# Constant products on TensorE before the first tile of x, the identity on SP's queue, and the norm's scale ahead of the weighted product at the end of a hybrid decoder layer

## The chip, the cores and the metric

The kernel runs on one core of one Trainium2 chip. The metric is the device time of one execution in microseconds. Before the change it is 662.05 us, the median of 3 runs (661.96 to 663.56).

A core has five engines that each work through their own list of instructions in order: TensorE (PE; its weight loads are shown as PEld), VectorE (DVE), ScalarE (ACT), GpSimd (POOL) and SyncE (SP), which here only issues DMAs. They wait for one another by semaphores.

## The reference

The layer has 512 rows of 1024 values in float32. What matters here is its first and last step:

```python
h = rms_norm(x, pre_mix_norm[l])
proj = jnp.einsum('bsd,dc->bsc', h, w_in[l])
...                       # MoBA attention and gated DeltaNet, output projection
x = x + rms_norm(mix, post_mix_norm[l])
h = rms_norm(x, pre_mlp_norm[l])
m = jnp.einsum('bsf,fd->bsd', jnp.square(jax.nn.relu(jnp.einsum('bsd,df->bsf', h, w_up[l]))), w_down[l])
x = x + rms_norm(m, post_mlp_norm[l])
```

with `rms_norm(x, w) = x * rsqrt(mean(x*x) + EPS) * w`. In the DeltaNet part, `exp(A_log)` enters the decay `g`.

## The kernel before

Every float32 factor of a large product is split into a high part (`hi`, a cast by ACT to a format that TensorE reads at one pass) and a low part (`lo`, the difference, by DVE or POOL); a product is then three matmuls, `hi*hi`, `hi*lo`, `lo*hi` (`mm3`).

**The start** (`pre_norm`). x comes in four tiles of 128 rows, 512 KB each (`take(0)` to `take(3)`, tensor `xx`). SP issues, in this order: x tile 0, the norm's weights (`pre_mix`, one row), x tile 1, two blocks of `w_in`, x tile 2, two more blocks of `w_in` (into `nb`), x tile 3, and then small constants, among them `alg` (`a_log`, line 312). The identity matrix that the transposes need is loaded by POOL (line 201). At most eight DMAs of SP are under way: each waits for the one eight before it.

TensorE first spreads the row of weights over 128 partitions, by a product with a row of ones (two matmuls into `ps_a`, the buffers `nb`). For each tile of x, ACT squares and sums the rows (line 214), POOL makes the root (`rstd_of`, lines 168 and 172), DVE scales by root and weights (line 220, `xs`), TensorE transposes eight 128x128 blocks (line 81, `ps_g`), ACT casts the high part out of PSUM (line 110, `hT_h`) and DVE subtracts to give the low part (line 111, `hT_l`), for two halves of the columns each. The scaling of tiles 0 and 1 stands ahead of the low parts of both in DVE's order. `ps_g` has three buffers, so the second half of tile 1 needs the first half of tile 0 to be done.

The projections (`projections`) begin with 48 matmuls for the first 256 rows: 24 for each of two output blocks. The weights for the second output block (`first_w[2]`, `first_w[3]`) are split after tile 2 and tile 3 of x have been squared: ACT's cast, and DVE's or POOL's subtraction (line 135). After that tiles 2 and 3 of x are transposed.

The order on TensorE is written out by `Weave`, which runs the stages as generators, counts up an estimated time `now` with every matmul, and starts a stage when its due time is reached (`START`, `WAIT`). In the first stage the order of ACT, DVE and POOL is held to the program's (`in_order`); between those, and later, a scheduler that simulates the engines places the other instructions. One of these is the exponential `ea<-alg` on ACT (line 466), which belongs to the DeltaNet's scalars and whose result is used later.

**The end.** The last product, of the MLP, is accumulated in PSUM. For each 128 rows `t` and half `b` of the columns, `half(b, t)` sums the squares on ACT (line 1308) and multiplies by the norm's weights `nb3` on DVE (line 1310 or 1312, result `Y(t, b)`). `normed_y(t)` adds the two sums (DVE, line 1316) and makes the root on POOL (lines 168, 172). `finish(t)` calls it if it has not been called, multiplies by the root, adds the residual (DVE, line 1326, twice) and issues the DMA of the output. Here the order of all engines is the program's (`ordered`). For the last two tiles computed (t = 0 and 1) the code is

```python
        half(1, j)
        finish(j)
```

so the order on DVE is: weighted product, sum, and the two final operations.

Of the kernel before, what the change touches and what calls it, by code (L numbers as in the profile page):

```python
# [20 lines left out]

RANK = {'chunks': 5, 'inverse': 3, 'scan': 3, 'scores': 4, 'values': 2, 'finish_o': 1, 'take': 4}
LEAD = {'chunks': 0, 'inverse': 100, 'scan': 100, 'scores': 0, 'values': 100, 'finish_o': 0, 'take': 0, 'take_a': 0}
START = (5.5, 9.0, 17, 16, 30, 10.5)
ORDER = "q0 k0 x0 k1 q1 q2 k2 k3 z0 q3 y0 x1 v0 w0 v1 y1 w1 v2 x2 v3 x3 y2 w2 y3 z1 w3 z2 z3"


class Weave:
# [10 lines left out]
    def spawn(self, rank, stream, lead=0):  # L39
        self.live.append([rank, self.now, stream, lead])  # L40
        self.live.sort(key=lambda s: s[0])

    def mark(self, name, wait=0.0):
        self.marks[name] = self.now + wait
# [22 lines left out]
def layer(ctx, tc, nc, x, w_in, w_ab, w_out, w_up, w_down, conv_w, a_log, dt_bias, gdn_norm_w, rel_bias,  # L67
# [8 lines left out]
    def mm(o, l, r, **kw):  # L76
        nc.tensor.matmul(o, l, r, **kw)  # L77
        weave.now += math.prod(r.shape[1:]) * (1 if r.dtype == FR else 4) / 2400

    def transpose(o, i, k=128):  # L80
        nc.tensor.transpose(o, i, ident[:k, :k])  # L81
        weave.now += k * 4 / 2400
# [18 lines left out]
    def big(name, shape=(128, 4, 512), dt=FT):  # L101
        return apool.tile(list(shape), dt, name=name, tag="big", bufs=14)
# [6 lines left out]
    def split(hi, lo, src):  # L109
        nc.scalar.copy(hi, src)  # L110
        tt(lo, src, f32(hi), op=OP.subtract)  # L111
# [20 lines left out]
    def ended(w, sub=None):  # L132
        hi, lo, raw, v = w
        nc.scalar.copy(hi, raw)  # L134
        (sub or tt)(lo, raw, f32(hi), op=OP.subtract)  # L135
        return v(hi), v(lo)
# [10 lines left out]
    ident = const.tile([128, 128], FT, name="ident")  # L147
# [7 lines left out]
    def bank(tag="g", shape=(128, 512)):  # L155
        return psum.tile(list(shape), FT, name="ps_" + tag, tag=tag, bufs={"mm": 2, "g": 3, "a": 3}[tag])
# [10 lines left out]
    def rstd_of(r, ss, n):  # L167
        nc.gpsimd.tensor_scalar(r, ss, 1.0 / n, EPS, op0=OP.mult, op1=OP.add)  # L168
        m = mhalf[:, :math.prod(r.shape[1:])]
        if len(r.shape) == 3:  # L170
            m = m.rearrange("p (a b) -> p a b", a=r.shape[1])
        nc.gpsimd.tensor_tensor(r, r, m, op=OP.pow)
        return r
# [3 lines left out]
    def bias_in():  # L177
        he = at.tile([128, 1280], FT, name="L")
        hot, es = he[:33, :640], he[:8, 640:]
        nc.sync.dma_start(hot, c_hot)  # L180
        rb = at.tile([33, 8], FT, name="rb", bufs=1)
        nc.vector.memset(rb, -1e30)
        nc.sync.dma_start(rb[:32], rel_bias)
        return hot, es, rb


    def pre_norm(ahead):
        one = tmp("one")[:1, :128]
        nc.vector.memset(one, 1.0)
        in_order.enter_context(tc.manual_schedule(engines={mybir.EngineType.Activation, mybir.EngineType.DVE, mybir.EngineType.Pool}))  # L190
        xx = [big("xx", (128, 2, 1024)) for _ in range(2)]
        nrow = nb0[:1]
        sqs = big("xs0", (128, 2, 1024))
        nb = [bank("a") for _ in range(2)]

        def take(t):
            nc.sync.dma_start(xx[t // 2][:, t % 2], x[128 * t:128 * t + 128, :])

        take(0)
        nc.sync.dma_start(nrow[:, :1024], pre_mix[None, :])  # L200
        nc.gpsimd.dma_start(ident, c_ident)
        take(1)
        ahead()
        take(2)
        ahead()
        take(3)
        rel.extend(bias_in())
        for b in range(2):
            mm(nb[b], one, nrow[:, 512 * b:512 * b + 512], start=True, stop=True)
        mark("x")  # L210

        def sumsq_x(t):
            ss = const.tile([128, 1], FT, name=f"ss{t}")
            act(sqs[:, t % 2], xx[t // 2][:, t % 2], AF.Square, accum_out=ss)
            return rstd_of(ss, ss, 1024)

        def scaled(t, r):
            for b in range(2):
                bs = slice(512 * b, 512 * b + 512)
                stt(sqs[:, t % 2, bs], xx[t // 2][:, t % 2, bs], r, nb[b], op0=OP.mult, op1=OP.mult)  # L220

        r = [sumsq_x(t) for t in range(2)]
        ahead()
        for t in range(2):
            scaled(t, r[t])
        for t in range(4):
            yield max(0, START[t] - weave.now)
            for b in range(2):
                tp = bank("g")
                for j in range(4):  # L230
                    transpose(tp[:, 128 * j:128 * j + 128], sqs[:, t % 2, 512 * b + 128 * j:512 * b + 128 * j + 128])
                v = tp.rearrange("p (a b) -> p a b", a=4)
                split(hT_h[b][:, :, 128 * t:128 * t + 128], hT_l[b][:, :, 128 * t:128 * t + 128], v)
            mark(f"h{t}", WAIT["h"])
            if t == 1:
                r = sumsq_x(2)
                first_w[2] = ended(first_w[2])
                scaled(2, r)
                r = sumsq_x(3)
                first_w[3] = ended(first_w[3], nc.gpsimd.tensor_tensor)  # L240
                scaled(3, r)
# [7 lines left out]
    def projections(items):  # L249
# [13 lines left out]
        for t in (0, 2):  # L263
# [5 lines left out]
            for i, ps in enumerate(first):  # L269
# [3 lines left out]
                if t:  # L273
                    spawn(RANK["take"], items[i][1](ps), LEAD["take"])
                yield 0
        W = [third, load(5)]
        for n in range(4, 2 * len(items)):
# [8 lines left out]
            for j in range(4):  # L286
                k = 4 * (n % 2) + j
                mm3(ps, hi[:, j], lo[:, j], kof(hT_h, k), kof(hT_l, k), k == 0, k == 7)
                if k == 7:
                    spawn(RANK["take"], ev(ps), LEAD["take_a" if col < 1536 else "take"])  # L290
                yield 0
# [6 lines left out]
    def tmp(name, dt=FT):  # L298
        return gpool.tile([128, 512], dt, name=name, tag="tmp", bufs=4)
# [9 lines left out]
    def constants_in():  # L309
        nc.sync.dma_start(cw, conv_w)  # L310
        nc.sync.dma_start(dtb, dt_bias.partition_broadcast(128))
        nc.sync.dma_start(alg, a_log.partition_broadcast(128))
        yield START[5]
        nc.vector.tensor_scalar(cw, cw, 0.5, None, op0=OP.mult)
# [271 lines left out]
    def bias():  # L586
        hot, es, rb = rel
        yield max(0, START[4] - weave.now)
        for a, b in ((0, 512), (512, 640)):
# [145 lines left out]
    def scan():  # L735
# [65 lines left out]
        for t in range(4):  # L801
# [38 lines left out]
            yield WAIT["state"]  # L840
            spawn(RANK["finish_o"], finish_o(t, o), LEAD["finish_o"])
        mark("scan")
# [4 lines left out]
    def finish_o(t, o):  # L847
        sq = tmp2("osq")
        act(sq, o, AF.Square)
        ss = sc.tile([128, 8], FT, name="oss")  # L850
        e8 = lambda a: a.rearrange("p (h e) -> p h e", h=8)
        nc.vector.tensor_reduce(ss, e8(sq), axis=mybir.AxisListType.X, op=OP.add)
        nc.gpsimd.tensor_tensor(ss, ss, rq2[:, t], op=OP.mult)
        r = rstd_of(ss, ss, 64)
        nc.gpsimd.tensor_tensor(r, r, rq8[:, t], op=OP.mult)
        tt(e8(o), e8(o), r[:, :, None].to_broadcast([128, 8, 64]), op=OP.mult)
        yield WAIT["o_in"]
        for p in range(4):
            yield f"z{p}"
        tp = bank(shape=(128, 4, 128))  # L860
        for p in range(4):
            transpose(tp[:, p], o[:, 128 * p:128 * p + 128])
        ts = slice(128 * t, 128 * t + 128)
        m = tmp2("om").rearrange("p (a b) -> p a b", a=4)
        stt(m, tp, nw, zss[0][:, :, ts], op0=OP.mult, op1=OP.mult)
        split(mx_h[1][:, :, ts], mx_l[1][:, :, ts], m)
        mark(f"o{t}", WAIT["o"])
# [148 lines left out]
    for p in range(4):  # L1016
        spawn(RANK["chunks"], chunks(p), LEAD["chunks"])
    spawn(RANK["inverse"], inverse(), LEAD["inverse"])
    spawn(RANK["values"], values(), LEAD["values"])
    spawn(RANK["scores"], scores(), LEAD["scores"])  # L1020
# [278 lines left out]
    def half(b, t):  # L1299
        bs = slice(512 * b, 512 * b + 512)  # L1300
        if (b, t // 2) != (1, 0):
            if (b, t) not in qs:
                summed(b, t)
            o = qs[b, t]
        else:
            o = C["R"][t]
        z = mu.tile([128, 512], FT, name="sq", tag="c", bufs=1)
        act(z, o, AF.Square, accum_out=ss[:, t, b:b + 1])
        if b:
            stt(Y(t, b), o, -1.0, nb3[:, bs], op0=OP.mult, op1=OP.mult)  # L1310
        else:
            tt(Y(t, b), o, nb3[:, bs], op=OP.mult)

    def normed_y(t):
        s1 = const.tile([128, 1], FT, name="s1", bufs=2)
        tt(s1, ss[:, t, 0:1], ss[:, t, 1:2], op=OP.add)  # L1316
        rs[t] = rstd_of(s1, s1, 1024)
# [30 lines left out]
    for t in (2, 3):  # L1348
        at_step(40, summed, 1, t)
        at_step(55, half, 0, t)  # L1350
# [90 lines left out]
```

## Time and profile before

| | us |
|---|---|
| median of 3 runs | 662.05 (661.96 to 663.56) |
| the profiled execution | 662.51 |
| its span, first to last instruction | 660.7 |
| TensorE busy | 632.4 |
| second tile of x landed | 7.50 |
| first 48 projection matmuls | 12.46 to 19.9 |
| last matmul ends | 653.43 |

The page and the answers of the trace give times from the span's start. A row of the timeline has the start, the duration, the engine, the line, the operation with output and inputs, and, in brackets, how long the engine was idle before it and what ended that. `x4` behind a row means that four records were merged. `SPq` is SP issuing a DMA. A chain of waits is followed back from the last instruction, at each step to what released it.

### The profile page before, as it was taken

The page shows a single profiled execution, that of the slowest core. Times are in us where ns is not written, and L with a number is a line of the kernel's source. Part 1 is how long each engine was busy: PE and PEld are TensorE (multiplying, and loading weights), DVE is VectorE, ACT ScalarE, POOL GpSimd, SP SyncE. Part 2 cuts the span into 40 slices and gives each one's busy share as a digit, 9 for nine tenths or more (in the row PEclk, how much of TensorE's full clock was granted, in tenths as well). Part 3 has the DMA queues.
Part 4 walks back from the last instruction along what each step waited for, and adds up shares of the span by engine and source line. Part 5 has one row for each costly group of instructions (what it writes and reads, how often), then busy time and mean ns, then how long its engine had stood idle before and what let it go on. Part 6 is the DMA issues. An engine that isn't in the chain of part 4 may idle for free.

```text
span 660.7 us, 11130 instructions
## 1 busy us (share of the span) xinstructions
PE 632.4 (96%) x4357; PEld 526.9 (80%) x4357; DVE 437.6 (66%) x627; ACT 360.5 (55%) x602; POOL 200.0 (30%) x231
## 2 busy tenths in 40 slices
PE   7899999899999999898999999999999999999995
PEld 4778777676687776676799899999998888887884
DVE  4358675997421335365445578878779888988775
ACT  5366564264636646854231675566566556665661
POOL 4355655332454236632302113111130130000002
PEclk9999999999999999999999999999999999999998
DMA  7232323223631202481249989899899999957503
GB/s 235 68 103 71 81 81 103 89 81 112 136 87 51 82 30 84 144 269 65 97 169 332 227 225 238 232 288 284 236 263 328 291 287 291 277 198 288 198 1 127
DMA packets 60226, 113.16 MB, mean 171 GB/s; under 512 B 15700, under 2 KB 34644, under 8 KB 59790
## 3 DMA queue, kind: packets, MB, share of 16 engines
q1 hardware_dynamic: 42446, 83.03, 36.4%
q0 software_dynamic: 17728, 29.43, 21.6%
q8 instruction: 34, 0.56, 0.3%
q14 instruction: 18, 0.15, 0.1%
HBM read 106.65 MB, written 35.15 MB: 215 GB/s over the span
## 4 chain that ended last, share of the span: by engine, by line
PE 80%; DVE 9%; ACT 5%; DMA 3%; POOL 1%; issue 1%; SPq 0%; DVEq 0%; POOLq 0%; ACTq 0%
PE ps_mm L77 41%; PE ps_g L77 21%; PE ps_a L77 14%; PE ps_a L81 2%; DVE conv L346 2%; PE ps_g L81 1%; DMA w_raw<-in_w_out 1%; DVE inv L726 1%; DVE pr L725 1%; DMA xx<-in_x 1%; DMA wd<-d_T 1%; DMA inv<-d_n 1%; ACT wo_h L122 1%; ACT ph L679 0%; DVE xs L948 0%
## 5 line engine op out<-in xcount | busy, mean ns | idle before, releaser
L135 POOL TENSOR_TENSOR w_lo<-w_raw,w_hi 128x512 fp32r<-128x512 f32 x54 | 70.7, 1311 | 116.1 <-ACT w_hi L134 115.8
L77 PE MATMUL ps_mm<-hT_h,w_hi 128*128 128x512 f32 (+1 forms) x224 | 93.1, 416 | 1.0 <-DVE conv L346 1.0
L77 PE MATMUL ps_mm<-hT_l,w_hi 128*128 128x512 f32 (+1 forms) x224 | 87.2, 389 | 0.0
L77 PE MATMUL ps_mm<-hT_h,w_lo 128*128 128x512 f32 (+1 forms) x224 | 86.7, 387 | 0.0
L110 ACT CAST wdh<-wd 128x1024 fp32r<-128x1024 f32 x53 | 55.9, 1054 | 52.0 <-PE ps_mm L77 23.5
L111 DVE TENSOR_TENSOR u_l<-w,u_h 128x1024 fp32r<-128x1024 f32 x46 | 56.2, 1224 | 37.8 <-ACT u_h L110 36.8
L111 DVE TENSOR_TENSOR wdl<-wd,wdh 128x1024 fp32r<-128x1024 f32 x53 | 64.9, 1225 | 22.8 <-ACT wdh L110 22.7
L110 ACT CAST u_h<-w 128x1024 fp32r<-128x1024 f32 x46 | 47.9, 1045 | 57.1 <-PE ps_a L77 19.7
L1123 POOL DMA_DIRECT2D d_T<-in_w_down x32 | 33.0, 1034 | 144.1 <-DMA d_T<-in_w_down 80.5
L134 ACT CAST w_hi<-w_raw 128x512 fp32r<-128x512 f32 x56 | 34.6, 620 | 46.0 <-PE ps_mm L77 26.2
L77 PEld LDWEIGHTS ps_mm<-hT_h,w_hi 128*128 128x128 f32 x224 | 42.8, 191 | 14.5 <-issue 6.3
L77 PEld LDWEIGHTS ps_mm<-hT_h,w_lo 128*128 128x128 f32 x224 | 43.0, 192 | 9.0
L77 PEld LDWEIGHTS ps_mm<-hT_l,w_hi 128*128 128x128 f32 x224 | 43.0, 192 | 6.4 <-DVE hT_l L111 0.2
L77 PE MATMUL ps_mm<-wdh,u_h 128*128 128x512 f32 x116 | 45.3, 390 | 0.0
L168 POOL TENSOR_SCALAR s<-s 128x1 f32<-128x1 f32 x12 | 3.8, 319 | 136.8 <-DVE s L1316 108.2
L77 PE MATMUL ps_mm<-wdl,u_h 128*128 128x512 f32 x116 | 45.1, 389 | 0.0
L77 PE MATMUL ps_mm<-wdh,u_l 128*128 128x512 f32 x116 | 45.1, 389 | 0.0
L346 DVE SCALAR_TENSOR_TENSOR conv<-ps_mm,cw,conv 128x511 f32<-128x511 f32 (+2 forms) x36 | 26.8, 745 | 18.0 <-ACT conv L343 17.5
L111 DVE TENSOR_TENSOR u_l<-f,u_h 128x1024 fp32r<-128x1024 f32 x28 | 34.1, 1219 | 0.0
L77 PE MATMUL ps_g<-wdh,u_h 128*128 128x512 f32 x80 | 31.2, 390 | 0.4 <-DVE y L1297 0.4
L651 DVE CUSTOM_DVE_ANT_0 L<-ps_a,E 128x512 f32<-128x512 f32 (+3 forms) x32 | 14.4, 487 | 25.7 <-PE ps_a L77 25.5
L77 PE MATMUL ps_g<-wdh,u_l 128*128 128x512 f32 x80 | 31.1, 389 | 0.0
(428 smaller groups left out, 1751.7 us busy)
## 6 DMA issues: line engine op xcount, KB each, us to landing
d_T<-in_w_down POOLq DMA_DIRECT2D x48, 512.0 KB, 10.6
wd<-d_T SPq DMA_DIRECT2D x32, 512.0 KB, 6.2
w<-in_w_up SPq DMA_DIRECT2D x28, 512.0 KB, 8.5
w_raw<-in_w_in SPq DMA_DIRECT2D x54, 256.0 KB, 2.6
wd<-in_w_down SPq DMA_DIRECT2D x24, 512.0 KB, 7.7
w_raw<-in_w_out SPq DMA_DIRECT2D x16, 256.0 KB, 2.7
d_T<-d_T POOLq DMA_DIRECT2D x8, 512.0 KB, 10.5
xx<-in_x SPq DMA_DIRECT2D x4, 512.0 KB, 6.6
```

Of the source, the lines that this page charges most:

```text
L77: nc.tensor.matmul(o, l, r, **kw)
L81: nc.tensor.transpose(o, i, ident[:k, :k])
L110: nc.scalar.copy(hi, src)
L111: tt(lo, src, f32(hi), op=OP.subtract)
L122: nc.scalar.copy(hi, raw)
L134: nc.scalar.copy(hi, raw)
L135: (sub or tt)(lo, raw, f32(hi), op=OP.subtract)
L346: stt(c[:, s:], p[:, :512 - s], cw[:, ft, j:j + 1], c[:, s:], op0=OP.mult, op1=OP.add)
L651: nc.vector.tensor_tensor_reduce(out=l, in0=s[hh][:, :w], in1=Es[hh][:, w - 1::-1], scale=1.0, scalar=3e38, op0=OP.add, op1=OP.min, accum_ ...
L725: tt(v, iN[:, 0:m, m:m + 1].to_broadcast([128, m, w]), iU[:, m:m + 1, m:32].to_broadcast([128, m, w]), op=OP.mult)
L726: tt(iU[:, 0:m, m:32], iU[:, 0:m, m:32], v, op=OP.subtract)
L1123: nc.gpsimd.dma_start(d_T[t][k], block(b, second)[k], accum_op=OP.add, max_dma_last_dim=1024)
```

## The change

Four edits. A constant tile of ones, 128x512 instead of one row of 128, is filled by DVE; TensorE multiplies its first 128 columns by themselves into a spare PSUM bank, seven times ahead of the spreading of the norm's weights, twice after it, and three times after the transposes of x tile 0. The identity is loaded by SP, behind x tile 1, instead of by POOL. At the end, for t = 0 and 1, `normed_y` is called between the sum of squares and the product with the weights. The estimated time of the planner also counts the added products.

```diff
+FILL = (7, 2, 3)
...
     def pre_norm(ahead):
-        one = tmp("one")[:1, :128]
-        nc.vector.memset(one, 1.0)
+        ones = tmp("one")
+        nc.vector.memset(ones, 1.0)
+        one = ones[:1, :128]
...
+        idle = bank("mm")
+
+        def busy(n, cols=128):
+            for _ in range(n):
+                mm(idle[:, :cols], ones[:, :128], ones[:, :cols], start=True, stop=True)
...
         take(0)
         nc.sync.dma_start(nrow[:, :1024], pre_mix[None, :])
-        nc.gpsimd.dma_start(ident, c_ident)
         take(1)
+        nc.sync.dma_start(ident, c_ident)
         ahead()
         take(2)
         ahead()
         take(3)
         rel.extend(bias_in())
+        busy(FILL[0])
         for b in range(2):
             mm(nb[b], one, nrow[:, 512 * b:512 * b + 512], start=True, stop=True)
+        busy(FILL[1])
...
             mark(f"h{t}", WAIT["h"])
+            if t == 0:
+                busy(FILL[2])
...
         act(z, o, AF.Square, accum_out=ss[:, t, b:b + 1])
+        if b and t < 2:
+            normed_y(t)
         if b:
             stt(Y(t, b), o, -1.0, nb3[:, bs], op0=OP.mult, op1=OP.mult)
```

The built program differs from the one before in these places on ACT, DVE, POOL and TensorE, and on SP by the identity's load and by two blocks of `w_in` that now stand ahead of the last part of the constant `c_sel`. On ACT, the exponential `ea<-alg` now stands between the casts of the first and of the second tile of x, where it stood behind the casts of the weights.

## The prediction

> **What bounds the kernel now.** I read the page first, then the chain of waits, then the timeline of its two ends, and last the order in which the changed program issues its instructions.
>
> The page: the engines' shares, and the row that shows the clock granted to TensorE (PEclk).
>
> ```profile
> span 660.7 us, 11130 instructions
> PE 632.4 (96%) x4357; PEld 526.9 (80%) x4357; DVE 437.6 (66%) x627; ACT 360.5 (55%) x602; POOL 200.0 (30%) x231
> PEclk9999999999999999999999999999999999999998
> ```
>
> TensorE is busy for 96% of the span, so whatever delays its first dense work delays nearly all that follows. The change touches only the first 20 us and the last 8. The chain of waits at the start:
>
> ```profile
> 1.55 5.95 DMA xx<-in_x
> 7.53 1.16 ACT xs L214 x2
> ...
> 9.04 0.56 POOL ss L172
> ...
> 9.63 1.41 DVE xs L220 x2
> 11.03 0.61 DVE hT_l L111
> ...
> 11.69 1.12 PE ps_g L81 x4
> 12.80 7.12 PE ps_mm L77 x48
> ```
>
> The second tile of x sets the start: it lands at 7.50 us, its squares, root and scaling take until 11.03, and the 48 products of the first half run from about 12.8 to 19.9. From 24 us on TensorE waits for no DMA; its longest waits are these:
>
> ```profile
> PE ps_a L81 <- DVE xs L954: 1.9, 2, 1.2
> PE ps_a L77 <- DVE mins L651: 1.7, 1, 1.7
> ```
>
> All are answers to TensorE's own earlier results. So I count a shift at 20 us as kept to the end.
>
> The timeline of the start (start, duration, engine, line):
>
> ```profile
> 4.12 3.75 PE L77 MATMUL ps_a<-nb,one 1*128 1x512 f32 x4 [4.12 <-DMA nb<-in_pre_mix]
> ...
> 7.80 2.03 PE L81 MATMUL ps_g<-ident,xs 128*128 128x128 f32 x8
> ...
> 9.61 1.06 ACT L110 CAST hT_h<-ps_g 128x512 fp32r<-128x512 f32 x2
> ...
> 10.10 0.33 SPq L312 DMA_DIRECT2D alg<-in_a_log  x1
> ...
> 10.95 1.94 DVE L111 TENSOR_TENSOR hT_l<-ps_g,hT_h 128x512 fp32r<-128x512 f32 x3
> ...
> 11.58 0.59 ACT L110 CAST hT_h<-ps_g 128x512 fp32r<-128x512 f32 x1 [0.91 <-PE ps_g L81]
> ...
> 12.84 0.59 ACT L110 CAST hT_h<-ps_g 128x512 fp32r<-128x512 f32 x1 [0.67 <-PE ps_g L81]
> 12.95 0.58 PE L77 MATMUL ps_mm<-hT_l,w_hi 128*128 128x256 f32 x1
> ...
> 13.46 0.69 DVE L111 TENSOR_TENSOR hT_l<-ps_g,hT_h 128x512 fp32r<-128x512 f32 x1 [0.57 <-ACT hT_h L110]
> ...
> 15.04 0.41 PE L77 MATMUL ps_mm<-hT_l,w_hi 128*128 128x256 f32 x1
> 15.25 0.36 PE L77 MATMUL ps_mm<-hT_h,w_lo 128*128 128x256 f32 x1
> ...
> 16.44 0.21 ACT L466 ACTIVATE ea<-alg 128x8 f32<-128x8 f32 x1
> 16.52 0.28 PE L77 MATMUL ps_mm<-hT_h,w_hi 128*128 128x256 f32 x1
> 16.64 0.28 PE L77 MATMUL ps_mm<-hT_l,w_hi 128*128 128x256 f32 x1
> ...
> 16.91 1.29 POOL L135 TENSOR_TENSOR w<-nb,w 128x512 fp32r<-128x512 f32 x1
> ...
> 19.64 0.29 PE L77 MATMUL ps_mm<-hT_h,w 128*128 128x256 f32 x1
> ```
>
> The reader is to see two things. A product of one shape is issued every 0.21 us at 15.04 and every 0.12 us at 16.52: TensorE runs at half rate until about 15.3, though PEclk reads 9 all along. And ACT's exponential of alg (line 466) stands at 16.44, long after alg was wanted by nobody. When alg lands (its DMA to landing, and what SP waited for):
>
> ```profile
> DMA to landing us min/median/max: 4.5/4.5/4.5
> SPq L312 <- DMA xx<-in_x: 0.9, 1, 0.9
> ```
>
> SP issued alg at 10.10, once an x tile (the third: SP keeps eight DMAs under way) had landed, and it landed 4.5 us later, at 14.6. Ahead of it in the same queue stand the fourth x tile and the other loads issued earlier.
>
> **The change part by part.**
>
> *Constant products.* DVE fills 128x512 ones instead of 1x128; its first scaling waits for ps_a (from 4.12 on), so nothing waits for the fill but TensorE's first filler. A filler is a quarter of the columns of one product on ps_a. Four records of ps_a took 3.75 us for two 512-column products, so a 128-column product takes 0.47 us at half rate. Seven take 3.3 us, from about 1.4 to 4.7; two take 0.9, three take 1.4. If the rate stays halved, the ps_a products end at 8.5 instead of 7.9, the first tile's transposes run from 9.4 to 11.4 behind two fillers, and three fillers reach 12.8; the second tile's transposes end at 15.0 (2.2 us for eight, from the chain's 1.12 for four). Without cover that is a loss of 15.0 - 12.8 = 2.2 us. If the rate doubles at about 5, all of it lies in the gap before the x tile, and the saving is that of the next paragraphs. The bounds of this part alone are thus -1.0 (below) and +2.2 us.
>
> Would the fillers raise the rate? TensorE was busy from 4.12 to 9.83 without a break and still ran at half rate at 15.04, so one-row products and transposes did not raise it; 2.8 us of full 128-row products from 12.46 to 15.25 did. Seven full-height fillers of 3.3 us are like the latter. [...]
>
> *Identity.* POOL loses one DMA issue; its roots wait for ACT's squares, so nothing is gained there. SP gains one issue of about 0.35 us (rows of this size: 0.33) ahead of both w_raw loads, the third and fourth x tile and all later loads. The same 64 KB go through the same engines. Value 0, bounds -0.3 (the 512 KB tile of x shares with nothing of POOL's) to +0.3 us (one issue later). The identity now lands about when x tile 1 does, 7.5, ahead of the transposes at 7.80. SP waits eight DMAs back, so alg still follows the third x tile.
>
> *An order that the diff does not show.* ACT's order in the changed program, from the two programs' lists:
>
> ```
> before: cast hT_h (4 times), squares, cast w, squares, cast w, ea<-alg, cast hT_h ...
> after:  cast hT_h, cast hT_h, ea<-alg [waits for alg's DMA], cast hT_h, cast hT_h, squares, cast w ...
> ```
>
> The exponential moved ahead of the casts of the second x tile, and ACT works in order. alg lands at 14.6, as before, for it stands in the same queue behind the same bytes (bounds 14.2 to 15.0). So the cast that started at 11.58 starts at 14.6 + 0.05 + 0.21 = 14.87, and the next (12.84 before) at 15.45, which is +2.6. Queued behind it on ACT: the squares of the third and fourth tile and two weight casts, all +2.6. DVE's low part of the second tile (the last of the three that end at 10.95 + 1.94 = 12.89) starts at 15.49 and ends at 16.18, so the second product on ps_mm moves from 12.95 to 16.2: +3.25.
>
> What follows depends on TensorE's rate at 16.2. (a) Half rate: again some 2.4 us at 0.21 before it doubles, as from 12.95 to 15.3, and the shift stays +3.25. (b) Full rate: 23 products of 0.12 bring the second set to 18.95. Its lower half needs the POOL row of 16.91, which moves from an end of 18.20 to 20.83; the product that reads it is the 15th, wanted at 18.95 + 14 x 0.12 = 20.63. So the last ten end at 20.83 + 1.2 = 22.05, where before the set ended at 19.64: +2.4.
>
> What the rate does in a stretch without products on ps_mm, TensorE's rows there:
>
> ```profile
> 19.76 1.47 PE L81 MATMUL ps_g<-ident,xs 128*128 128x128 f32 x12
> 21.76 0.66 PE L81 MATMUL ps_g<-ident,xs 128*128 128x128 f32 x4 [0.53 <-DVE hT_l L111]
> 24.11 0.39 PE L77 MATMUL ps_g<-hT_h,abw 128*32 128x512 f32 x1 [1.69 <-DVE two L443]
> 24.34 0.39 PE L77 MATMUL ps_g<-hT_l,abw 128*16 128x512 f32 x1
> ```
>
> From 19.76 to 24.11 there were only transposes and gaps, and the rate held (the next product follows 0.23 us behind, with twice the columns). But the new hole, from the transposes' end near 12.3 to 15.5, is 3.2 us without any work; TensorE's longest waits after the start are 1.9 us in total for two and 1.7 for one, so no row shows a rate that outlives it, and the kernel begins at half rate from rest. I take (a).
>
> If the fillers never raised the rate, the stall covers them: the transposes would end at 15.0, before the cast's 15.45. So (a) stands either way.
>
> *The end.* The timeline after the last product:
>
> ```profile
> 653.51 0.60 ACT L1308 ACTIVATE sq<-ps_mm 128x512 f32<-128x512 f32 x1 [4.75 <-PE ps_mm L77]
> ...
> 654.24 0.69 DVE L1310 SCALAR_TENSOR_TENSOR y<-ps_mm,nb 128x512 f32<-128x512 f32 x1 [0.25 <-ACT sq L1308]
> 654.84 0.15 DVE L1316 TENSOR_TENSOR s<-ssy 128x1 f32<-128x1 f32 x1
> 655.08 0.19 POOL L168 TENSOR_SCALAR s<-s 128x1 f32<-128x1 f32 x1 [2.54 <-DVE s L1316]
> 655.36 0.55 POOL L172 TENSOR_TENSOR s<-s,mhalf 128x1 f32<-128x1 f32 x1
> 655.94 1.42 DVE L1326 SCALAR_TENSOR_TENSOR y<-y,s,xy 128x512 f32<-128x512 f32 x2 [0.95 <-POOL s L172]
> ```
>
> Now the sum s comes first on DVE (it waits for ACT's square as y did, 654.24), then y. POOL starts at 654.24 + 0.24 (the time from s to POOL before: 654.84 to 655.08) = 654.48 and line 1326 follows 0.86 later (655.08 to 655.94 before), at 655.34; y ends at about 655.1, hidden. That is 655.34 instead of 655.94: -0.6. The new wait delays only y on DVE, and y is no longer last. Bounds -0.7 (all of y) to -0.4 (s at its full 0.15 and one more issue). For the third to fourth tile the order is the old one; the first tile's move is under TensorE's products.
>
> *Sum.* +3.25 - 0.6 = +2.65. The profiled execution took 662.51, 0.46 above the median, and its span 660.7; the sum is a difference read in it, and I add it to the median: 662.05 + 2.65 = 664.7 us. About 0.3%, 2.0 us, is what a measurement of this kernel tells from no change.
>
> **The rivals.**
> 1. The rate rises early and outlives the hole: (b), 2.4 - 0.6 = +1.8, 663.85. For it: the rate held from 19.76 to 24.11. Against: that stretch had 2.1 us of transposes in it. [...]
> 2. Other side, one mechanism: alg is there before ACT reaches the exponential (about 10.7). Then nothing stalls, and with fillers that work the products start as before at 12.95 at full rate; ACT's casts come 0.5 earlier by the faster transposes, the POOL row ends at 17.7, and the set ends at 17.7 + 1.2 = 18.9 instead of 19.64: -0.75, at most -1.0 if that row does not bind. With -0.6: 660.7 (660.45). It decides from alg's landing: each microsecond before 14.6 gives one back, and at about 12 the whole change is even. Against it: alg is issued only after the third x tile and behind the fourth, in one queue.
> 3. The change does not do what it says: no stall, and the rate never rises. Then fillers and transposes stand in the way, +2.2 - 0.6 = +1.6, 663.65.
>
> **How the numbers follow.** Forecast 0.70; rival 1 0.17; rival 2 0.08; rival 3 0.05. The half-rate time in (a) may end some 0.6 us earlier or later than before (the three runs of before themselves spread by 1.6 us), so (a) reaches from 664.0 to 665.4. Down to rival 3's 663.65 and rival 1's less 0.5, and up by alg's +0.4, the range is 663.2 to 665.6. Slower by over 0.3% (above 664.04): 0.85 of (a), four tenths of rivals 1 and 3, some 0.70. Faster by over 0.3% (under 660.06): rival 2 with every bound in its favour, and what I haven't seen, 0.08. Within: 0.22.
>
> **What would show it.** Right: ea<-alg at about 14.6 with ACT idle some 3.9 us before it, released by alg's DMA; the casts of the second tile at 14.9 and 15.4; products every 0.21 us for some microseconds after 16; POOL's root of the last tile beside y, and line 1326 some 0.6 us nearer to the last product. Rival 1: products every 0.12 us at 16.2. Rival 2: ea about 10.7, and no idle time. Rival 3: ps_a ending near 8.5. The forecast is wrong if alg lands early, if the shift is taken back after 24 us, or if the load order, one DMA longer, makes a later weight late.

## The result, and the profile after

The changed kernel takes 665.36 us, the median of 20 runs (663.37 to 668.43); the kernel before took 662.12 in the same series (660.34 to 663.78). The ratio is 1.0048, with a 95% interval of 1.0035 to 1.0060: slower by 3.2 us (2.3 to 4.0). The forecast was 664.7, with a range of 663.2 to 665.6. The time is as forecast. The way there is only in part.

The profiled execution of the changed kernel took 663.78 us, 1.27 more than that of before (662.51); its span is 662.0 instead of 660.7. It is one of the faster of the 20, so the traces of this pair show 1.3 of the 3.2 us. Lines of the changed kernel are numbered one higher up to line 187, by 2 to 9 up to line 209, and by 10 to 14 behind that.

The start, from its timeline:

```profile
1.48 3.35 PE L78 MATMUL ps_mm<-one 128*128 128x128 f32 x14 [1.48 <-DVE rb L183]
...
4.77 3.78 PE L78 MATMUL ps_a<-nb,one 1*128 1x512 f32 x4
...
5.47 1.06 ACT L224 ACTIVATE xs<-xx 128x1024 f32<-128x1024 f32 x1 [0.31 <-DMA xx<-in_x]
...
8.47 1.22 PE L78 MATMUL ps_mm<-one 128*128 128x128 f32 x4
...
9.49 1.91 PE L82 MATMUL ps_g<-ident,xs 128*128 128x128 f32 x8
...
11.20 1.49 PE L78 MATMUL ps_mm<-one 128*128 128x128 f32 x6
...
12.48 1.51 PE L82 MATMUL ps_g<-ident,xs 128*128 128x128 f32 x8
12.78 0.21 ACT L478 ACTIVATE ea<-alg 128x8 f32<-128x8 f32 x1 [0.75 <-DMA alg<-in_a_log]
...
13.57 1.08 ACT L111 CAST hT_h<-ps_g 128x512 fp32r<-128x512 f32 x2 [0.59 <-PE ps_g L82]
...
14.94 0.39 PE L78 MATMUL ps_mm<-hT_l,w_hi 128*128 128x256 f32 x1 [0.34 <-DVE hT_l L112]
...
15.16 0.28 PE L78 MATMUL ps_mm<-hT_h,w_lo 128*128 128x256 f32 x1
...
15.28 0.28 PE L78 MATMUL ps_mm<-hT_h,w_hi 128*128 128x256 f32 x1
```

TensorE has no gap from 1.48 to the end of the second tile's transposes at 13.99, and works at half rate nearly all that time: two records make a filler, and the first fourteen took 3.35 us, 0.48 us a filler; the last six, at 11.20, 0.50. Only the products from 15.16 on follow one another by 0.12 us. The exponential of alg waited on ACT, as forecast, but for 0.75 us and until 12.78; the casts behind it then waited 0.59 us more, for TensorE. x tile 1 had landed by 5.47, two microseconds earlier than in the trace of before, and the second product still starts at 14.94 instead of 12.95.

The end, from the timeline:

```profile
655.45 0.60 ACT L1320 ACTIVATE sq<-ps_mm 128x512 f32<-128x512 f32 x1 [4.75 <-PE ps_mm L78]
...
656.17 0.16 DVE L1330 TENSOR_TENSOR s<-ssy 128x1 f32<-128x1 f32 x1 [0.85 <-ACT sq L1320]
656.24 0.68 DVE L1324 SCALAR_TENSOR_TENSOR y<-ps_mm,nb 128x512 f32<-128x512 f32 x1
656.41 0.19 POOL L169 TENSOR_SCALAR s<-s 128x1 f32<-128x1 f32 x1 [2.55 <-DVE s L1330]
656.69 0.55 POOL L173 TENSOR_TENSOR s<-s,mhalf 128x1 f32<-128x1 f32 x1
657.27 1.42 DVE L1340 SCALAR_TENSOR_TENSOR y<-y,s,xy 128x512 f32<-128x512 f32 x2 [0.35 <-POOL s L173]
```

From the square to the last pair of operations it is 657.27 - 655.45 = 1.82 us, and was 655.94 - 653.51 = 2.43: -0.61.

Between the two ends the shift doesn't stay what it was. The same instructions in both traces, first before (the row of 24.11 stands in the prediction), then after (TensorE's rows of the timeline):

```profile
277.39 0.66 PE L81 MATMUL ps_a<-ident,R 128*128 128x128 f32 x4 [0.63 <-ACT ph L679]
...
280.45 0.63 PE L81 MATMUL ps_g<-ident,ot 128*128 128x128 f32 x4 [1.09 <-DVE ot L856]
```

```profile
25.12 0.39 PE L78 MATMUL ps_g<-hT_h,abw 128*32 128x512 f32 x1 [1.69 <-DVE two L455]
...
279.14 0.66 PE L82 MATMUL ps_a<-ident,R 128*128 128x128 f32 x4 [1.62 <-ACT ph L691]
...
282.41 0.63 PE L82 MATMUL ps_g<-ident,ot 128*128 128x128 f32 x4 [1.30 <-DVE ot L868]
```

The shift is +1.0 us at 25, +0.5 at 255 (the same product at 255.02 and 255.49), +1.75 at 279, where TensorE waits 1.62 us instead of 0.63 for ACT, and +1.96 at 282. From there it stays to the last product, and the end takes 0.6 back. What makes ACT late at 279 is a load of the output projection's weights (`w_raw<-in_w_out`, the ninth of sixteen). Its issue on SP, the cast on ACT that waits for it, the subtraction of the same block on POOL and SP's next run of issues, before and after:

```profile
268.57 2.04 SPq L121 DMA_DIRECT2D w_raw<-in_w_out  x2
...
271.66 0.62 ACT L122 CAST wo_h<-w_raw 128x512 fp32r<-128x512 f32 x1
...
272.35 1.28 POOL L123 TENSOR_TENSOR wo_l<-w_raw,wo_h 128x512 fp32r<-128x512 f32 x1 [2.11 <-ACT wo_h L122]
...
273.66 6.45 SPq L121 DMA_DIRECT2D w_raw<-in_w_out  x4
```

```profile
269.33 2.04 SPq L122 DMA_DIRECT2D w_raw<-in_w_out  x2
...
273.37 1.26 ACT L123 CAST wo_h<-w_raw 128x512 fp32r<-128x512 f32 x2 [0.86 <-DMA w_raw<-in_w_out]
...
274.07 1.29 POOL L124 TENSOR_TENSOR wo_l<-w_raw,wo_h 128x512 fp32r<-128x512 f32 x1 [3.07 <-ACT wo_h L123]
...
275.39 6.68 SPq L122 DMA_DIRECT2D w_raw<-in_w_out  x4
```

From issue to cast it is 3.1 us before and 4.0 after. The delay is handed on whole: the cast is 1.71 us later than before, the subtraction 1.72, the next issue 1.73, and TensorE's row of 277.39 is 1.75 later. The view of the DMA queues of the changed kernel, from 269.3 to 273.4 (q8 is the queue that the profile names instruction):

```profile
q1 hardware_dynamic: 647, 0.86, 70.0%
q8 instruction: 1, 0.02, 1.5%
w_raw<-in_w_out SPq DMA_DIRECT2D x2, 256.0 KB, 3.0
```

One packet of 16 KB on the instruction queue lies inside the load's time. In the trace of before that packet came at 272.6, behind the load. Over the whole trace of before this queue has 34 packets of 16384 bytes (0.56 MB), against TensorE's 8714 records, one packet for 256; from one packet to the next TensorE starts 148 to 381 of them, 253 in the mean, and no other engine ever more than 55 instructions.

### The profile page after: what moved, and what is told of

The parts are those of the page before. It is cut to its first block, busy times and chain, and to the rows that moved or that the text cites. A ratio compares the mean times of both kernels' runs of the same rounds, so it can differ in the third digit from the quotient of the medians.

```text
span 662.0 us, 11179 instructions
## 1 busy us (share of the span) xinstructions
PE 635.9 (96%) x4381; PEld 531.2 (80%) x4381; DVE 438.5 (66%) x627; ACT 360.9 (55%) x602; POOL 199.4 (30%) x230
## 4 chain that ended last, share of the span: by engine, by line
PE 82%; DVE 8%; ACT 4%; DMA 3%; POOL 2%; issue 1%; DVEq 0%; POOLq 0%; ACTq 0%; SPq 0%
PE ps_mm L78 42%; PE ps_g L78 21%; PE ps_a L78 14%; PE ps_a L82 2%; DMA w_raw<-in_w_out 2%; PE ps_g L82 2%; DVE conv L358 1%; DVE pr L737 1%; DVE inv L738 1%; DMA inv<-d_n 1%; DMA wd<-d_T 1%; POOL wo_l L124 1%; ACT wo_h L123 0%; DVE xs L960 0%; POOL s L173 0%
```

## The experiments

All times are in microseconds, each ratio against runs of the kernel before on the same chip (662.78, 662.09 and 662.29 us for the three series).

**The kernel before once more**, to see what differs from one execution to the next.

> The kernel before, unchanged, for a second trace of it: ratio 1.000 by every theory. [...]

662.53 us, ratio 0.999 (0.997 to 1.001). x tile 1's square starts at 6.84 here, 7.53 in the first trace; over fourteen traces of all kernels it lay between 5.5 and 8.1, and alg landed between 12.8 and 14.6. TensorE's rate rose at 13.6 here and at 15.4 in the first trace; half-clock stretches of 3.41 us came at 23.8 and 262.7 here, at 261.2 there. These are properties of an execution. The prediction had taken them from one, as properties of the kernel.

**Only the end.**

```diff
         act(z, o, AF.Square, accum_out=ss[:, t, b:b + 1])
+        if b and t < 2:
+            normed_y(t)
         if b:
```

> The kernel before with only the sum and the root ahead of the weighted product. All theories: 0.6 us faster (ratio 0.9991); from the start of the last square to line 1326's start 1.82 us instead of 2.43. If something else at the end binds, 0.

661.20 us, ratio 0.9982 (0.9961 to 1.0002). In the trace, 651.37 to 653.19, again 1.82 us. The part does what was forecast in the trace; in the time, the forecast 0.9991 lies in the interval, and so does 1.

**Only the identity.**

```diff
-        nc.gpsimd.dma_start(ident, c_ident)
         take(1)
+        nc.sync.dma_start(ident, c_ident)
```

> The kernel before with only the identity's load moved from POOL to SP, behind x tile 1. Prediction: 0 (-0.3 to +0.3 us). Rival, from the trace after (x tile 1 landed at 5.47 instead of 7.50): the load from POOL had held up x tile 1; then it lands near 5.5 here too, the chain of squares, root and scaling comes up to 2.0 us earlier, as far as the one-row products (end 7.87) allow, and the time falls by 1 to 2 us.

661.34 us, ratio 0.9982 (0.9966 to 0.9999). x tile 1's square starts at 7.09, not near 5.5 as the rival wanted. Over all traces it starts at 5.6 to 8.1 with the identity on POOL (eight traces) and at 5.5 to 7.1 with it on SP (six), so where the identity is loaded does not decide it. No loss is seen; whether the part brings something, up to some 2 us, the interval leaves open, and by what way too.

**Only the fillers** (with the move of `ea<-alg` that the scheduler makes of them).

> The kernel before with only the fillers (seven, two, three), the identity on POOL, the old end; the scheduler moves ea<-alg ahead here too. Theory of the prediction (ACT's wait for alg): x tile 1 and alg land late as before, ACT waits for alg until about 14.6, products from about 16.2, time +2.4 to +3.3 us. Rival (the fillers themselves, at half rate, push the one-row products and the transposes back): ps_a ends near 8.5, transposes of the second tile end near 15, ACT does not wait for alg but for TensorE, time about +2.2 us. Rival (the fillers raise the rate at about 5 us): ps_a ends near 7.

666.27 us, ratio 1.0048 (1.0032 to 1.0065): the loss of the whole change is in this part. The timeline:

```profile
12.48 1.73 PE L82 MATMUL ps_g<-ident,xs 128*128 128x128 f32 x8
...
13.89 0.21 ACT L478 ACTIVATE ea<-alg 128x8 f32<-128x8 f32 x1 [1.86 <-DMA alg<-in_a_log]
14.01 1.05 ACT L111 CAST hT_h<-ps_g 128x512 fp32r<-128x512 f32 x2
...
15.35 0.38 PE L78 MATMUL ps_mm<-hT_l,w_hi 128*128 128x256 f32 x1 [0.34 <-DVE hT_l L112]
```

Here alg, at 13.89, is last, and ACT waits for it for 1.86 us; but the transposes behind the fillers run until 14.2 too. The two causes lie beside each other, and the next but one run parts them.

**The change without fillers.**

```diff
-FILL = (7, 2, 3)
+FILL = (0, 0, 0)
```

> The changed kernel with no fillers (0, 0, 0); the identity on SP and the end as changed; ea<-alg stands behind the weights' casts again. From the single parts: 0 from the identity, -0.6 us from the end, so about 0.9991 of before. If the fillers had brought anything, this would be slower than that by as much.

661.49 us, ratio 0.9986 (0.9972 to 0.9999). Without fillers the loss is gone; the interval lies just below 1.

**The change with `ea<-alg` put back.**

```diff
                 first_w[3] = ended(first_w[3], nc.gpsimd.tensor_tensor)
+                act(ea_, alg, AF.Exp)
...
-        ea = gpool.tile([128, 8], FT, name="ea")
-        act(ea, alg, AF.Exp)
+        ea = ea_
```

> The changed kernel with all its fillers, and ea<-alg put back behind the weights' casts on ACT; no other instruction moves. If ACT's wait for alg alone makes the loss (the prediction): the whole 3.2 us of loss goes and the time is about 0.6 us under before. If the fillers at half rate make it as well (in the trace after, the second tile's transposes end only when ACT's wait is over): the second tile's casts still start near 13.6, released by TensorE, and at most 0.5 us of the loss goes.

664.71 us, ratio 1.0038 (1.0025 to 1.0051). The waits of ACT from 9 to 15 us:

```profile
ACT hT_h L111 <- PE ps_g L82: 3.6, 3, 2.1
```

ACT now waits for TensorE alone, the casts start at 13.33, and most of the loss stays. So with the fillers in place, the wait for alg decides little.

**Only the move of `ea<-alg`**, no fillers.

```diff
             mark(f"h{t}", WAIT["h"])
+            if t == 0:
+                act(ea_, alg, AF.Exp)
```

> The kernel before, without fillers, with ea<-alg alone moved ahead of the second tile's casts (one pair of small DVE operations far behind it changes places too). Prediction's mechanism: ACT waits for alg until 13.9 to 14.6, the casts start at 14.1 to 14.9 instead of 11.6, the second product on ps_mm comes 2 to 3 us later than in the kernel before, time +2 to +3 us. If alg lands by 12, or the lost time is made up by 25 us: under +0.5 us.

665.74 us, the median of seven runs, ratio 1.0064 (1.0037 to 1.0090): +4.2 us, more than forecast, though the interval (2.4 to 6.0) reaches into the forecast. The timeline:

```profile
13.50 0.21 ACT L236 ACTIVATE ea<-alg 128x8 f32<-128x8 f32 x1 [3.13 <-DMA alg<-in_a_log]
13.62 1.06 ACT L110 CAST hT_h<-ps_g 128x512 fp32r<-128x512 f32 x2
...
14.24 0.43 PE L77 MATMUL ps_mm<-hT_h,w_hi 128*128 128x256 f32 x1 [2.83 <-ACT hT_h L110]
...
14.96 0.29 PEld L77 LDWEIGHTS ps_mm<-hT_l,w_hi 128*128 128x128 f32 x1 [0.54 <-DVE hT_l L111]
14.96 0.58 PE L77 MATMUL ps_mm<-hT_l,w_hi 128*128 128x256 f32 x1 [0.29 <-DVE hT_l L111]
...
15.56 0.41 PE L77 MATMUL ps_mm<-hT_h,w_hi 128*128 128x256 f32 x1
...
15.77 0.41 PE L77 MATMUL ps_mm<-hT_l,w_hi 128*128 128x256 f32 x1
```

ACT waits 3.13 us and TensorE 2.83. Behind that hole the products follow one another by 0.21 us until 17.7: the rate had risen at 11.0 and was halved from 14.4 to 17.8. The mechanism of the prediction is real and, alone, costs as much as the whole change. In the changed kernel it lies beside the fillers' time.

**Five fillers only, all done before the norm's weights land**, and `ea<-alg` put back.

```diff
-FILL = (7, 2, 3)
+FILL = (5, 0, 0)
```

> The changed kernel with ea<-alg put back and only five fillers ahead of ps_a (0.47 us each, so they end near 3.9, before the norm's weights land at 4.1), none behind. If it is the fillers behind 4.1 us that cost: no loss left, -0.6 us of the end, about 0.9991. [...]

664.68 us, ratio 1.0040 (1.0022 to 1.0057): the expectation failed. Nothing is in the way at the start (the second product starts at 12.06), and the kernel is as slow as with twelve fillers. So neither the wait for alg nor the fillers' time at the start can be the whole cause. In this trace, too, the ninth load of w_out was late: 4.8 us from issue to cast, with the instruction packet 1.9 us behind the issue.

That left two suspects that every kernel with fillers shares: more instructions on TensorE, and the spare PSUM buffer, which swaps the two `ps_mm` buffers for all that follows.

**Five, then twelve products of 1x1** in the kernel before: instructions without work.

```diff
         rel.extend(bias_in())
+        idle = nb[0]
+        for _ in range(5):
+            mm(idle[:1, :1], one[:, :1], one[:, :1], start=True, stop=True)
```

> The kernel before with five 1x1 products more, ahead of the one-row products, which cost TensorE next to nothing and lie before the norm's weights land; with their weight loads they are 20 records more of TensorE's program, as five fillers are. Theory (instruction loads): TensorE's instructions are fetched in blocks of 16 KB, one per some 256 instructions; with 20 more ahead the block that came 4.0 us behind the ninth load of w_out (268.6 to 272.6) comes 2 us earlier, inside that load, whose landing then takes 4 to 5 us instead of 3; the stage from 268 to 283 us is 1 to 1.5 us longer, the time +1.5 to +2.5 us. If the fillers cost by their work or their rate: 0.

> As the run before, with twelve 1x1 products (48 records, as the twelve fillers). Theory of the instruction loads: the block comes some 1.5 to 2 us behind the ninth load of w_out, as in the changed kernel, time +1.5 to +2.5 us. Otherwise 0.

664.86 us, ratio 1.0032 (1.0012 to 1.0053), and 664.11, ratio 1.0024 (1.0011 to 1.0038). The timeline of the first:

```profile
1.07 0.39 PE L77 MATMUL ps_a<-one 1*1 1x1 f32 x10 [1.07 <-DVE rb L182]
3.92 3.78 PE L77 MATMUL ps_a<-nb,one 1*128 1x512 f32 x4 [2.47 <-DMA nb<-in_pre_mix]
...
268.75 2.04 SPq L121 DMA_DIRECT2D w_raw<-in_w_out  x2
...
273.46 0.62 ACT L122 CAST wo_h<-w_raw 128x512 fp32r<-128x512 f32 x1 [1.54 <-DMA w_raw<-in_w_out]
```

Products of 0.39 us in all, done 2.47 us before the next has its data, make the kernel 2.1 us slower, and what is late in the trace is the ninth load: 4.7 us from issue to cast. The expectation of the instruction loads holds in the packet, the load and the time; the stage behind it grew by more than was expected (table below).

**The spare buffer**, with a single 1x1 product.

```diff
+        idle = bank("mm")
+        for _ in range(1):
+            mm(idle[:1, :1], one[:, :1], one[:, :1], start=True, stop=True)
```

> The kernel before with the spare PSUM buffer of the fillers allocated (which swaps the two ps_mm buffers for all that follow) and one 1x1 product into it (4 records). If the swap of the buffers makes the loss at 277 to 283 us: +1 to +2 us. By the theory of the instruction loads: 4 records move the block by less than 0.5 us, and the time is that of before, within 0.5 us.

663.55 us, ratio 1.0013 (0.9996 to 1.0029). The time alone doesn't settle it. In the trace the ninth load is as before: issue at 268.41, cast at 271.65, 3.2 us. The swap of the buffers doesn't make the late load. The expectation missed in one thing: four records moved the packet not by less than 0.5 us but from 4.1 to 2.3 us behind the issue.

**The work of five fillers in two products**, 8 records in place of 20, with `ea<-alg` put back as in the run of five.

```diff
-        busy(FILL[0])
+        busy(1, 512)
+        busy(1)
```

> The changed kernel with ea<-alg put back and, in place of five fillers of 128 columns ahead of ps_a, one of 512 and one of 128: the same work and rate, 8 records in place of 20. By the theory of the instruction loads the block stays within 1 us of where it was in the kernel before, and the loss of the five fillers (+2.6 us) shrinks by 1 us or more; if their work costs, the time stays at +2.6 us.

662.70 us, ratio 1.0000 (0.9983 to 1.0017), against 1.0040 (1.0022 to 1.0057) with five in another series: the same work with fewer instructions is some 2.6 us faster. But the packet did not stay where it was; it came 1.3 us behind the ninth load's issue, and that load took 4.4 us. The expectation was wrong in that. What was spared in this trace are the fourth and the fifth load (2.7 and 2.6 us from issue to cast, where five fillers had 3.6 and 3.1). So a late ninth load need not show in the time: here its stage costs 1.4 us (table), the end gives 0.6 back, and the 0.8 us that is left lies within the interval of the time (-1.1 to +1.1).

The ninth load over all traces, from the records of SP, ACT and the instruction queue, and the stage around it. The last column says how much longer than in the first trace TensorE takes from its product at 255.02 to its transposes at 280.45 (the same two instructions in every trace):

| kernel | packet behind the issue, us | issue to cast, us | stage longer by, us |
|---|---|---|---|
| before (two traces) | 4.1, 3.9 | 3.1, 3.2 | 0, 0.2 |
| end only, identity only, no fillers | 4.2, 4.0, 4.0 | 3.2, 3.1, 3.1 | 0.0, 0.2, 0.0 |
| `ea<-alg` moved | 4.2 | 3.1 | 0.3 |
| spare buffer | 2.3 | 3.2 | 0.2 |
| after, fillers only, `ea<-alg` put back | 1.5, 1.9, 1.8 | 4.0, 4.4, 4.3 | 1.5, 2.1, 3.6 |
| five fillers, five in two products | 1.9, 1.3 | 4.8, 4.4 | 2.7, 1.4 |
| 1x1 products, five and twelve | 1.4, 1.3 | 4.7, 3.9 | 2.2, 1.5 |

The packet falls 1.3 to 1.9 us behind the issue in seven of the fourteen traces, those whose TensorE program is at least eight records longer, and just there the load is 0.7 to 1.7 us late and the stage 1.4 to 3.6 us longer, against 0.3 at most in the others. How far the packet moves does not go by the number of records: 4, 8, 20 and 48 of them bring it to 2.3, 1.3, 1.4 to 1.9 and 1.3 to 1.9.

The traces also show what is late in the load. The ninth load leaves sixteen completions, semaphore updates, in each trace. Fifteen of them have come by 2.9 to 3.2 us after the issue in all fourteen traces. The sixteenth comes with them (3.0 to 3.2) where the packet is not in the way; in the seven late traces it comes alone, at 3.8 to 4.8, and each time 1.53 to 1.55 us after the end of the instruction packet. In the changed kernel the fifteenth comes at 272.48, the packet ends at 271.82, and the sixteenth comes at 273.35. It is this one completion that ACT's cast of 273.37 waits for, and with it the stage.

Half-clock stretches differ between executions as well. The granted clock of the run with five 1x1 products, in three stretches (columns: busy time and count of each engine, then PEclk, DMA share and GB/s):

```profile
262.30:265.60 3.30, 3.30 (x21) 2.33 (x21) 2.30 (x5) 2.74 (x8) 2.98 (x4) 0.50 0.25 89
266.00:279.00 13.00, 11.42 (x93) 7.94 (x91) 2.52 (x8) 9.65 (x21) 7.22 (x7) 1.00 0.43 142
279.35:282.70 3.35, 3.35 (x16) 3.21 (x16) 1.35 (x2) 2.19 (x4) 2.42 (x3) 0.50 0.24 78
```

In twelve of the fourteen traces a stretch at half clock lies near 262 (3.4 us long, 6.8 in one); here a second one follows TensorE's longer wait at 279. Only this one of the seven late traces has a stretch there. Other traces have one at 14, 24 or 132 us, besides or instead, and the second trace of the kernel before is among them. That the late load brings such stretches is not shown.

Over the executions the mean granted clock was 0.995 in the median for the kernel before, 0.995 to 0.9965 for the kernels with the end, the identity or both, 0.992 and 0.994 with the five and twelve 1x1 products, 0.9955 with five fillers in two products, and 0.989 to 0.9935 for the changed kernel and the three others with fillers of 128 columns only; a stretch of 3.41 us at half clock takes 0.0026 off the mean (half of 3.41 in 660.7), and the slower executions of a kernel are mostly those with the lower clock. In the changed kernel the eight executions with 0.994 or more took 663.4 to 664.5 us, the other twelve 665.3 to 668.4. With five 1x1 products the five executions with 0.994 or more have a median of 662.3, no more than the kernel before has in the same series at that clock (662.2, thirty executions); with twelve, seven such executions have 664.0. So the five products' loss lies mostly in executions with a lower clock, and whether the ninth load was late in the others is not known. The late load itself was traced at 0.995 too, in the changed kernel and with five fillers in two products.

## Why the prediction was right in time and only partly in its reasons

*The time and its sign.* 665.36 lies within 663.2 to 665.6, near its upper end; the shift was +3.2 where +2.65 was forecast. That the time fell into the range is in part luck: the start, forecast at +3.25, gave about +1, and a stage at 255 to 280 us that the sum does not have gave 1.5 to 3.6 us in the three traces with twelve fillers.

*The order of ACT, and its wait.* Right as a mechanism: the move alone costs 4.2 us (2.4 to 6.0), and in the run with the fillers alone ACT's wait of 1.86 us stands ahead of the casts. Wrong as the term of the sum. The step "alg lands at 14.6, as before (bounds 14.2 to 15.0)" took one execution's landing for the kernel's: over fourteen traces it was 12.8 to 14.6. And the step "If the fillers never raised the rate, the stall covers them" stands the other way round in the profiled execution: the fillers cover the stall. With `ea<-alg` put back, 0.0038 (0.0025 to 0.0051) of the 0.0048 stay.

*The rate.* "Would the fillers raise the rate?" It did not rise early in any trace with fillers: it rose at 13.4 in the changed kernel, 13.9, 12.9 and 13.7 in three others. The prediction's reading of one trace, that one-row products and transposes do not raise the rate and 128-row products do, does not hold over fourteen: the rate rose between 11.0 and 16.9, and in two traces without fillers (end only, `ea<-alg` moved) at 11.1 and 11.0, at the transposes and ahead of the first 128-row product (11.39 and 14.24). Case (a) then fell with its hole: TensorE was busy until 13.99 and reached the products at full rate, as in (b). Where the hole did come, with `ea<-alg` moved alone, the rate behind it was halved, as (a) says. So the forecast's +3.25 at the start was not there; the pair of traces shows +1.0 at 25 us. The trace of before is a late one in that: the second trace of the same kernel stands 0.9 us earlier there.

*What was counted as kept.* "So I count a shift at 20 us as kept to the end" failed. The waits were all answers to TensorE's results, as read, but some of those answers wait for a load on the way (ACT's cast for w_out), and that load moved by itself. The term that is missing in the sum is the 48 records that the fillers add to TensorE's program: +1.5 us in the pair of traces from 255 to 280 us, and, as 1x1 products without any work, 1.6 us (0.7 to 2.5) and 2.1 us (0.8 to 3.5) of the whole time.

*The identity, and the end.* 0 and -0.6 were forecast. The identity alone is no loss (0.9982, 0.9966 to 0.9999); the end took 1.82 us instead of 2.43, as worked out, and 1.82 or 1.83 in all six traces that have it (2.42 or 2.43 in the eight others).

*The rivals.* Rival 3's "+2.2" by fillers at half rate is nearer to what the start shows than the forecast: ps_a ends at 8.55 and the transposes at 13.99, where it had 8.5 and 15.0. Rival 1's early rise of the rate and rival 2's early alg (about 10.7) did not come: the changed kernel's trace has 13.4 and 12.8.

*What adds up and what does not.* At 255 us the three traces with twelve fillers stand 0.3 to 0.9 us behind the first trace of before, and the eight traces without fillers and without the moved exponential stand from 2.1 us ahead of it to 0.2 behind; the means are 1.0 us apart. The stage to 280 us adds 1.5, 2.1 and 3.6 us in the three, and the end gives 0.6 back. With the stage's mean of 2.4 that is an estimate of +2.8, from three traces, where +3.2 (2.3 to 4.0) was measured. How much of it the half-clock stretches make is open: no execution of the changed kernel with a low clock was profiled. Five fillers ahead of the weights cost as much (1.0040) as twelve (1.0038), although their products start 2.6 us earlier in the traces (12.06 to 14.69). The granted clock tells them apart: the three executions with five and a clock of 0.994 or more took 662.4 to 663.5, the six with twelve 663.9 to 664.7, and the median of the five comes from the nine others (664.1 to 667.3). Why those are so many is open.

## What to carry to other kernels

An edit can cost in other places than its own instructions, and here it did. Read the changed order of every engine for waits that moved ahead: here an exponential before four casts, alone 4.2 us (2.4 to 6.0). Count the instructions that an edit adds to the longest program: here 4 to 48 records more on TensorE brought a 16 KB packet of the instruction queue nearer to the issue of a load, from some 4 us behind it to 2.3 with 4 records and to 1.3 to 1.9 with 8 to 48, not in proportion to their number. Look for the load that a stage waits for: in the seven traces whose packet came 1.3 to 1.9 us behind its issue, it landed 0.7 to 1.7 us later, and the stage was 1.4 to 3.6 us longer. And a landing time from one trace is a sample (alg's lay between 12.8 and 14.6 in fourteen): take a second trace of the same kernel before a sum rests on it.

## What was not expected of the hardware

TensorE was busy from 1.48 to 13.44 us without a gap, with full-height fillers, one-row products and transposes in turn, and stayed at half rate (0.48 to 0.50 us a filler). Over fourteen traces the rise came between 11.0 and 16.9 us, with fillers between 12.9 and 13.9; no trace shows that fillers bring it forward, and what sets the moment is open. In both traces of the pair the half-clock stretch near 262 us is 3.41 us long.

The 16 KB packet on the instruction queue delayed the ninth load, of 256 KB, by 0.7 to 1.7 us where it fell 1.3 to 1.9 us behind its issue, though it is one packet among some 600 in that time, and takes about 1 us (0.98 by its record; 1.5% of the time of 16 DMA engines in 4.1 us, above). Fifteen of the load's sixteen completions are in time and one comes 1.53 to 1.55 us after the packet's end, in all seven late traces; why this one alone is late is open, for the records do not name the DMA engine of a packet.
